# Products by columns in a two-layer decoder trunk: three products of 256 columns per k tile, or one of 512 and one of 256 with a join

## The chip, the cores and the metric

The kernel runs on one core of one Trainium2 chip. The metric is device time in microseconds of that core, median of several runs. The engines are named as the profile names them: PE (TensorE matmul), PEld (its weight loads), DVE (VectorE), ACT (ScalarE), POOL (GpSimd) and SP (SyncE, which issues the DMAs here).

## What is computed

The reference is a decoder trunk of two layers on x of 256 tokens by 1024 features, all in float32.

```python
for i in range(DEPTH):                      # DEPTH = 2
    y = chunked_gmlp(x, ...) if i % 2 == 0 else moba_attention(x, ...)
    x = layer_norm(DN_ALPHA * x + y, ln_mix_g[i], ln_mix_b[i])
    y = conv_ffn(x, f_w_up[i], f_conv_w[i], f_conv_b[i], f_w_down[i])
    x = layer_norm(DN_ALPHA * x + y, ln_ffn_g[i], ln_ffn_b[i])

# chunked_gmlp: z = gelu(x @ w_in); u, v = split(z); v = layer_norm(v); mix v over positions; (u * v) @ w_out
# moba_attention: q, k, v = x @ w_qkv; 16 heads of 64; softmax with a position bias; @ w_o
# conv_ffn: h = x @ w_up (1024 to 5632); causal convolution of width 3; gelu(g) * val; @ w_down
```

## The kernel before

**Two parts of every operand.** Each weight and each x is split into a high part (rounded to the matmul's fp32r) and a low part (what the rounding left). A product is three matmuls: high by high, high by low, low by high. For weights, ACT writes `whi` and DVE writes `wlo` from a raw chunk in SBUF; for x the tiles are `xth` and `xtl`, kept transposed (128 features of a k tile on the partitions, tokens along them); there are KT = 8 k tiles.

**The stream of weights.** 1 MB chunks come in the order a_v, a_u, a_out, f_up0 (22 chunks), f_dn0 (11), b_v, b_qk (8), b_o, f_up1, f_dn1, through two raw buffers, and each is split into two sub-chunks of 1024 columns. The rings of high and low parts hold five chunks; a chunk is fetched and split when PE has spent the one five before it (`spent`, L376).

**By rows and by columns.** Some stages work by rows (`rows_step`, L520): x is the stationary operand, 512 columns of the weights move, and the result has tokens on the partitions. The others work by columns (`cols_times`, L528): a 128 x 128 piece of the weights is stationary, the 256 tokens of x move, and 256 columns of one PSUM bank collect one block of 128 output features, over 8 k tiles of three matmuls each. By columns go a_u (8 blocks), chunks 2 to 21 of each f_up (two blocks each, gate and value) and b_qk (two blocks for each of 8 pairs of heads). PSUM has eight banks, taken in turn; each block of columns takes one.

**What reads a block.** In a_u (L639) ACT applies Gelu from PSUM. In f_up, `gate` (L655) reads each block three times in PSUM: ACT Identity with bias and scale (the first tap), and two scalar_tensor_tensor on DVE (the other taps); then Gelu on ACT, a product on DVE, and a split by ACT and DVE into `rr`. In b_qk, `project` (L735) makes from the bank a copy of the first 128 tokens, a high part (ACT) and a low part (DVE); scores, softmax, transposes and the products with v follow for a pair some pairs behind.

**What sets the order.** The kernel records all operations and then orders them itself (`Plan.emit`, L122): a list scheduler with a cost for every operation gives each engine its fixed order, which the engine then works through first in, first out. PE's long products keep the recorded order; transposes and the attention's small products fill in between. Operations of DVE and ACT are taken by due time. Numbers of the cost model are not times of the chip.

The layout of the transposed x before is (t, k, c): tokens in two halves t of 128, in each the 8 k tiles. A moving operand of 256 tokens is therefore read in two runs of 128.

Of the kernel before, what the change touches and what calls it, by code (L numbers as in the profile page):

```python
# [11 lines left out]
F32 = mybir.dt.float32  # L12
F32R = mybir.dt.float32r
# [210 lines left out]
def trunk_kernel(ctx: ExitStack, tc: tile.TileContext, a: dict, out: bass.AP):  # L224
# [13 lines left out]
    xth, xtl = Ring(tiles("xth", 1, KT * S, F32R)), Ring(tiles("xtl", 1, KT * S, F32R))  # L238
# [154 lines left out]
    def xt_view(b):  # L393
        return b.ap.rearrange("p (t k c) -> p t k c", t=NT, k=KT)
# [3 lines left out]
    xv32 = xT32.ap.rearrange("p (t k c) -> p t k c", t=NT, k=KT)  # L398

    def load_xt(k, n, rank):  # L400
        load(xv32[:, :, k:k + n, :], a["xT"][:, :, k:k + n, :], [(xT32, [(t, j) for t in range(NT) for j in range(k, k + n)])],
             rank=rank)
        for t in range(NT):
            parts = [(t, j) for j in range(k, k + n)]
            split((xh, parts, xt_view(xh)[:, t, k:k + n, :]), (xl, parts, xt_view(xl)[:, t, k:k + n, :]),
                  (xT32, parts, xv32[:, t, k:k + n, :]), by="dve" if k == 0 else "act")
# [188 lines left out]
    def gmlp():  # L595
# [37 lines left out]
        for g in range(GROUPS):  # L633
# [5 lines left out]
            act(us[g].ap, b.ap[:, :S], AF.Gelu_apprx_tanh, [b], [us[g]], psum=True, table="gelu")  # L639
# [7 lines left out]
    def conv_up(layer, h, l):  # L647
# [58 lines left out]
    def moba(h, l, scr):  # L706
# [5 lines left out]
        qkring = [Places("ff", (j * 2 * P, j * 2 * P + P), P) for j in range(2)]  # L712
# [22 lines left out]
        def project(i, j):  # L735
# [4 lines left out]
            src, (th, tl) = b.ap[:, at2:at2 + n], (x.new() for x in qkparts[j])  # L740
            act(t.ap, b.ap[:, :P], AF.Copy, [b], [t], scale=scale, psum=True)
# [178 lines left out]
```

## Time and profile before

| | us |
|---|---|
| timed runs | 584.77, 582.66, 583.03 |
| median | 583.03 |
| span of the profiled execution, first to last instruction | 580.6 |
| PE busy / DVE busy / ACT busy in it | 565.9 / 453.5 / 340.9 |

The page gives the span of the profiled execution and no other time of it; the median of the timed runs lies 2.4 us above that span. TensorE's granted clock has a mean of 0.996 of full speed.

Rows of groups read: line, engine, operation, out<-in by tile names, shapes, count, then busy us, mean ns of one, idle time of the engine before them and what ended it. Rows of the timeline read: start, duration, engine, line, operation, count; x4 are four in a row merged into one line. PE's matmuls are pipelined and drawn longer than the distance from one to the next, so starts are to be compared, not lengths. Rows of the windows read: stretch, its length, busy us (and count) of PE, PEld, DVE, ACT and POOL, granted clock, DMA share, GB/s. Rows of waits read: engine, tile and line, what it waited for, us in total, times, longest.

PE's stages in the profiled execution are about: a_v to 31, a_u to 57, a_out with its LayerNorm to 81, f_up0 to 210 (by columns from 93), f_dn0 to 271, b_v to 293, b_qk to 358, b_o to 385, f_up1 to 513 (by columns from 397), f_dn1 to 573.

### The profile page before, as it was taken

The page shows a single profiled execution, that of the slowest core. Times are in us where ns is not written, and L with a number is a line of the kernel's source. Part 1 is how long each engine was busy: PE and PEld are TensorE (multiplying, and loading weights), DVE is VectorE, ACT ScalarE, POOL GpSimd, SP SyncE. Part 2 cuts the span into 40 slices and gives each one's busy share as a digit, 9 for nine tenths or more (in the row PEclk, how much of TensorE's full clock was granted, in tenths as well). Part 3 has the DMA queues.
Part 4 walks back from the last instruction along what each step waited for, and adds up shares of the span by engine and source line. Part 5 has one row for each costly group of instructions (what it writes and reads, how often), then busy time and mean ns, then how long its engine had stood idle before and what let it go on. Part 6 is the DMA issues. An engine that isn't in the chain of part 4 may idle for free.

```text
span 580.6 us, 9855 instructions
## 1 busy us (share of the span) xinstructions
PE 565.9 (97%) x3850; PEld 521.7 (90%) x3850; DVE 453.5 (78%) x845; ACT 340.9 (59%) x620; POOL 11.2 (2%) x17
## 2 busy tenths in 40 slices
PE   6999999999999999999999999999999999999994
PEld 4799889999999998888899988889999999988884
DVE  4599889988989874448978988889989888874326
ACT  5556567866676654325667875577767766653200
POOL 0020010000000000001000000000000000000001
PEclk9999999999999999999999999999999999999998
DMA  7997536667555555450665542416755654545202
GB/s 254 345 346 279 189 128 217 222 214 266 194 200 213 196 205 201 171 208 23 242 268 176 182 164 73 148 71 227 290 209 218 215 189 179 207 163 210 73 1 72
DMA packets 20138, 111.01 MB, mean 191 GB/s; under 512 B 2251, under 2 KB 6268, under 8 KB 7676
## 3 DMA queue, kind: packets, MB, share of 16 engines
q1 hardware_dynamic: 20092, 110.39, 52.9%
q8 instruction: 30, 0.49, 0.3%
q14 instruction: 16, 0.13, 0.1%
HBM read 109.31 MB, written 1.07 MB: 190 GB/s over the span
## 4 chain that ended last, share of the span: by engine, by line
PE 93%; DMA 3%; DVE 1%; ACT 1%; issue 1%; SPq 0%; DVEq 0%; ACTq 0%
PE bank L293 91%; DMA raw<-in_a_v 2%; PE bank L299 2%; DMA raw<-in_b_o 1%; ACT whi L305 1%; DVE wlo L311 1%; DVE x L315 0%; SPq L322 0%; ACT rr L305 0%; DVE ff L773 0%; ACT ff L305 0%; DVE stat L461 0%; DVEq L916 0%; DVE qk L315 0%; ACT qk L305 0%
## 5 line engine op out<-in xcount | busy, mean ns | idle before, releaser
L311 DVE TENSOR_TENSOR wlo<-raw,whi 128x1024 fp32r<-128x1024 f32 (+1 forms) x212 | 229.8, 1099 | 56.6 <-ACT whi L305 56.1
L305 ACT ACTIVATE whi<-raw 128x1024 fp32r<-128x1024 f32 (+1 forms) x212 | 196.3, 956 | 79.6 <-PE bank L293 52.1
L293 PE MATMUL bank<-xth,whi 128*128 128x256 f32 x832 | 237.1, 285 | 0.0
L293 PE MATMUL bank<-xth,wlo 128*128 128x256 f32 x832 | 235.4, 283 | 0.0
L293 PE MATMUL bank<-xtl,whi 128*128 128x256 f32 x832 | 235.4, 283 | 0.0
L293 PEld LDWEIGHTS bank<-xth,whi 128*128 128x128 f32 x832 | 159.5, 192 | 1.5 <-issue 0.6
L293 PEld LDWEIGHTS bank<-xtl,whi 128*128 128x128 f32 x832 | 159.6, 192 | 0.2
L293 PEld LDWEIGHTS bank<-xth,wlo 128*128 128x128 f32 x832 | 159.6, 192 | 0.0
L293 PE MATMUL bank<-whi,rr 128*128 128x512 f32 (+1 forms) x528 | 152.9, 371 | 0.0
L293 PEld LDWEIGHTS bank<-whi,rr 128*128 128x128 f32 x528 | 96.4, 188 | 16.6
L293 PE MATMUL bank<-wlo,rr 128*128 128x512 f32 (+1 forms) x264 | 97.7, 370 | 0.0
L315 DVE SCALAR_TENSOR_TENSOR ff<-bank,convc,ff 128x254 f32<-128x254 f32 (+1 forms) x176 | 80.5, 476 | 13.9 <-ACT ff L305 12.9
L305 ACT ACTIVATE ff<-bank,convc 128x256 f32<-128x256 f32 x88 | 48.7, 561 | 48.7 <-PE bank L293 37.2
L293 PEld LDWEIGHTS bank<-wlo,rr 128*128 128x128 f32 x264 | 49.8, 189 | 8.2
L293 PE MATMUL bank<-whi,xth 128*128 128x512 f32 x96 | 39.1, 408 | 5.4 <-DVE xth L328 5.0
L293 PE MATMUL bank<-wlo,xth 128*128 128x512 f32 x96 | 38.6, 402 | 1.0 <-DVE wlo L311 0.9
L293 PE MATMUL bank<-whi,xtl 128*128 128x512 f32 x96 | 38.1, 397 | 0.0
L305 ACT ACTIVATE ff<-bank,lncol 128x128 f32<-128x128 f32 x48 | 18.9, 459 | 28.7 <-PE bank L299 28.7
L315 DVE SCALAR_TENSOR_TENSOR x<-x,bank 128x512 f32<-128x512 f32 (+1 forms) x24 | 14.3, 596 | 25.0 <-PE bank L293 24.9
L293 PEld LDWEIGHTS bank<-whi,xth 128*128 128x128 f32 x96 | 18.5, 193 | 9.4 <-ACT whi L305 5.8
L293 PEld LDWEIGHTS bank<-wlo,xth 128*128 128x128 f32 x96 | 18.4, 192 | 5.7 <-DVE wlo L311 2.4
L305 ACT ACTIVATE rr<-ff 128x256 fp32r<-128x256 f32 x52 | 21.1, 407 | 2.8 <-DVE ff L311 2.7
(51 smaller groups left out, 350.6 us busy)
## 6 DMA issues: line engine op xcount, KB each, us to landing
raw<-in_f_up SPq DMA_DIRECT2D x44, 1024.0 KB, 4.8
raw<-in_f_dn SPq DMA_DIRECT2D x22, 1024.0 KB, 4.8
raw<-in_b_qk SPq DMA_DIRECT2D x8, 1024.0 KB, 4.8
lnrow<-in_lnrow SPq DMA_DIRECT2D x5, 1024.0 KB, 7.2
raw<-in_a_u SPq DMA_DIRECT2D x4, 1024.0 KB, 5.4
raw<-in_a_out SPq DMA_DIRECT2D x4, 1024.0 KB, 5.2
raw<-in_b_v SPq DMA_DIRECT2D x4, 1024.0 KB, 4.7
raw<-in_b_o SPq DMA_DIRECT2D x4, 1024.0 KB, 5.1
```

Of the source, the lines that this page charges most:

```text
L293: nc.tensor.matmul(o, l, x, start=start, stop=stop)
L299: nc.tensor.transpose(o, x, ident.ap)
L305: plan.op("act", ns, lambda: nc.scalar.activation(o, x, func, **kw), r, w, table=table)
L311: dve(70 + 1.04 * flat(x), lambda: nc.vector.tensor_tensor(o, x, y, op=op), r, w)
L315: lambda: nc.vector.scalar_tensor_tensor(o, x, s, y, op0=op0, op1=op1), r, w)
```

## The change

The high and low parts of the transposed x become the two halves of one tile `xt2`, and its layout becomes (k, t, c), so that the 256 tokens of a k tile lie together. In `cols_times` one matmul of 512 columns multiplies the high weights with both parts of x: high by high falls into the first half of the bank and high by low into the second. A matmul of 256 columns adds low by high into the first half. A new helper, `join`, brings the halves together in SBUF: ACT copies the second half, DVE adds the first (with a scale for q). Gelu in a_u, the three taps in f_up (chunks 2 to 21) and the splits in b_qk then read the joined block in SBUF; `hring` is a ring of eight places for the blocks of f_up. In b_qk the kept block is 256 wide instead of 128. xT is loaded in the new layout, with one split for both halves of the tokens. Work by rows is as before, with the new view of x.

```diff
+    xt2 = sb.tile([P, 2 * KT * S], F32R, name="xt2")
+    xth, xtl = Ring([xt2[:, :KT * S]]), Ring([xt2[:, KT * S:]])
+    xboth = xt2.rearrange("p (x k s) -> p x k s", x=2, k=KT)
...
-        return b.ap.rearrange("p (t k c) -> p t k c", t=NT, k=KT)
+        return b.ap.rearrange("p (k t c) -> p t k c", t=NT, k=KT)
...
-        for t in range(NT):
-            parts = [(t, j) for j in range(k, k + n)]
-            split((xh, parts, xt_view(xh)[:, t, k:k + n, :]), (xl, parts, xt_view(xl)[:, t, k:k + n, :]),
-                  (xT32, parts, xv32[:, t, k:k + n, :]), by="dve" if k == 0 else "act")
+        parts, sl = [(t, j) for t in range(NT) for j in range(k, k + n)], slice(k * S, (k + n) * S)
+        load(xT32.ap[:, sl], a["xT"][:, sl], [(xT32, parts)], rank=rank)
+        split((xh, parts, xh.ap[:, sl]), (xl, parts, xl.ap[:, sl]), (xT32, parts, xT32.ap[:, sl]),
+              by="dve" if k == 0 else "act")
...
     def cols_times(b, h, l, hi, lo):
-        o = b.ap[:, :S].rearrange("p (t c) -> p t c", t=NT)
-        hv, lv = xt_view(h), xt_view(l)
+        both = b.ap.rearrange("p (x s) -> p x s", x=2)
         for k in range(KT):
             ks, parts = slice(k * P, (k + 1) * P), [(t, k) for t in range(NT)]
-            mms([(o, w.ap[:, ks], x[:, :, k, :], k == 0 and j == 0, k == KT - 1 and j == 2)
-                 for j, (w, x) in enumerate([(hi, hv), (hi, lv), (lo, hv)])],
+            mms([(both, hi.ap[:, ks], xboth[:, :, k, :], k == 0, False),
+                 (b.ap[:, :S], lo.ap[:, ks], xboth[:, 0, k, :], False, k == KT - 1)],
                 [(hi, [k // 2]), (lo, [k // 2]), (h, parts), (l, parts)], [b])
...
+    def join(b, c, scale=1.0):
+        act(c.ap, b.ap[:, S:], AF.Copy, [b], [c], scale=scale, psum=True)
+        if scale == 1.0:
+            tt(c.ap, b.ap[:, :S], c.ap, ALU.add, [b, c], [c])
+        else:
+            stt(c.ap, b.ap[:, :S], scale, c.ap, ALU.mult, ALU.add, [b, c], [c])
...
-            act(us[g].ap, b.ap[:, :S], AF.Gelu_apprx_tanh, [b], [us[g]], psum=True, table="gelu")
+            join(b, us[g])
+            act(us[g].ap, us[g].ap, AF.Gelu_apprx_tanh, [us[g]], [us[g]], table="gelu")
...
-                srcs.append((b, b.ap[:, :S]))
+                c = hring.new()
+                join(b, c)
+                srcs.append((c, c.ap))
...
-            act(t.ap, b.ap[:, :P], AF.Copy, [b], [t], scale=scale, psum=True)
-            act(th.ap, src, AF.Copy, [b], [th], scale=scale, psum=True)
-            stt(tl.ap, src, scale, th.ap.bitcast(F32), ALU.mult, ALU.subtract, [b, th], [tl])
+            join(b, t, scale)
+            th, tl = (x.new() for x in qkparts[j])
+            split((th, [0], th.ap), (tl, [0], tl.ap), (t, [0], t.ap[:, at2:at2 + n]))
```

**How the fixed orders move.** The first place is DVE's queue in the middle of f_up0, about one chunk. `wlo` are low parts of later weights, `convc` marks the taps of the convolution, `ff<-ff` is the product of gate and value, `rr` its low part. Before:

```order
L311 TENSOR_TENSOR wlo6_81<-raw0_85,whi6_71 128x1024
L311 TENSOR_TENSOR ff_105<-ff_105 128x256
L311 TENSOR_TENSOR wlo7_82<-raw0_85,whi7_72 128x1024
L315 SCALAR_TENSOR_TENSOR ff_105<-bank0_106,convc_117,ff_105 128x255
L315 SCALAR_TENSOR_TENSOR ff_105<-bank1_107,convc_117,ff_105 128x255
L315 SCALAR_TENSOR_TENSOR ff_105<-bank0_106,convc_117,ff_105 128x254
L315 SCALAR_TENSOR_TENSOR ff_105<-bank1_107,convc_117,ff_105 128x254
```

And in the changed kernel, where `ff<-bank7,ff` and `ff<-bank0,ff` are the additions of two joins:

```order
L313 TENSOR_TENSOR wlo6_81<-raw1_86,whi6_71 128x1024
L313 TENSOR_TENSOR wlo7_82<-raw1_86,whi7_72 128x1024
L313 TENSOR_TENSOR ff_104<-bank7_112,ff_104 128x256
L317 SCALAR_TENSOR_TENSOR ff_104<-ff_104,convc_116 128x255
L313 TENSOR_TENSOR rr_103<-ff_104,rr_103 128x256
L313 TENSOR_TENSOR ff_104<-bank0_105,ff_104 128x256
L317 SCALAR_TENSOR_TENSOR ff_104<-ff_104,convc_116 128x254
```

Each block now has an addition that reads the bank, and the taps name the bank no more; the taps of a block stand further behind its product on PE.

The second place is DVE's queue as a_u begins, where the LayerNorm of v (`stat`, `lnrow`) and the first spatial products (`ff<-bank,ff` before) stand. Before:

```order
L311 TENSOR_TENSOR ff_105<-bank0_106,ff_105 128x256
L315 SCALAR_TENSOR_TENSOR ff_105<-ff_105,stat0_92,lnrow0_91 128x512
L315 SCALAR_TENSOR_TENSOR ff_105<-ff_105,stat1_93,lnrow0_91 128x512
L311 TENSOR_TENSOR ff_105<-ff_105 128x256
L315 SCALAR_TENSOR_TENSOR ff_105<-ff_105,stat0_92,lnrow0_91 128x256
L315 SCALAR_TENSOR_TENSOR ff_105<-ff_105,stat1_93,lnrow0_91 128x256
L311 TENSOR_TENSOR ff_105<-bank4_110,ff_105 128x256
L311 TENSOR_TENSOR wlo6_81<-raw0_85,whi6_71 128x1024
```

And in the changed kernel, where banks 4 to 7 are the first four blocks of a_u and bank 0 the first spatial product:

```order
L313 TENSOR_TENSOR ff_104<-bank4_109,ff_104 128x256
L313 TENSOR_TENSOR ff_104<-bank5_110,ff_104 128x256
L313 TENSOR_TENSOR ff_104<-bank6_111,ff_104 128x256
L313 TENSOR_TENSOR ff_104<-bank7_112,ff_104 128x256
L313 TENSOR_TENSOR ff_104<-bank0_105,ff_104 128x256
L317 SCALAR_TENSOR_TENSOR ff_104<-ff_104,stat0_91,lnrow0_90 128x512
L317 SCALAR_TENSOR_TENSOR ff_104<-ff_104,stat1_92,lnrow0_90 128x512
L313 TENSOR_TENSOR ff_104<-ff_104 128x256
L313 TENSOR_TENSOR wlo6_81<-raw0_85,whi6_71 128x1024
```

Four additions stand together ahead of the rest of the LayerNorm and of the first low part of a_out; the other four of a_u stand between later rows.

The third place is ACT's queue in b_qk, around the blocks of one pair of heads. `qk256` and `qk128` are high parts of k and of q, `smax` marks the exponentials, `rr<-bank` the high parts of transposed weights of the softmax. Before:

```order
L305 ACTIVATE ff_105<-bank4_110 128x128
L305 ACTIVATE qk25601_124<-bank4_110 128x256
L305 ACTIVATE rr_104<-bank5_111 128x384
L305 ACTIVATE rr_104<-bank6_112 128x384
L305 ACTIVATE whi3_68<-raw0_85 128x1024
L305 ACTIVATE whi4_69<-raw1_86 128x1024
L305 ACTIVATE qk12800_119<-bank0_106 128x128
L305 ACTIVATE ff_105<-bank0_106 128x128
```

And in the changed kernel:

```order
L307 ACTIVATE ff_104<-bank4_109 128x256
L307 ACTIVATE rr_103<-bank5_110 128x384
L307 ACTIVATE qk25601_123<-ff_104 128x256
L307 ACTIVATE rr_103<-bank6_111 128x384
L307 ACTIVATE whi2_67<-raw0_85 128x1024
L307 ACTIVATE ff_104<-bank0_105 128x256
L307 ACTIVATE whi3_68<-raw0_85 128x1024
L307 ACTIVATE qk12800_118<-ff_104 128x128
```

The high part no longer stands beside the copy out of the bank: it waits for DVE's addition, and another operation of ACT stands between the two.

More of the change, by code (lines that the diff above doesn't have):

```diff
@@ L237, in trunk_kernel @@
     raws = Ring(tiles("raw", RAWS, CH))
-    xth, xtl = Ring(tiles("xth", 1, KT * S, F32R)), Ring(tiles("xtl", 1, KT * S, F32R))
+    xt2 = sb.tile([P, 2 * KT * S], F32R, name="xt2")
+    xth, xtl = Ring([xt2[:, :KT * S]]), Ring([xt2[:, KT * S:]])
+    xboth = xt2.rearrange("p (x k s) -> p x k s", x=2, k=KT)
     xs_ = tiles("x", NT, D)
@@ L651, in conv_up @@
         gring, yring = Places("ff", (4 * S, 5 * S), S), Places("ff", (6 * S, 8 * S), HALF)
+        hring = Places("ff", (3456, 3712, 3968, 4224, 6 * S, 7 * S, 8 * S, 9 * S), S)
         cc = convc.ap.rearrange("p (n f c) -> p n f c", n=DEPTH, c=4)
@@ L658, in gate @@
                 cw, c = cc[:, layer, j * FT + i, :], cring[j].new()
-                act(c.ap, o, AF.Identity, [b, convc], [c], bias=cw[:, 3:4], scale=cw[:, 2:3], psum=True)
+                act(c.ap, o, AF.Identity, [b, convc], [c], bias=cw[:, 3:4], scale=cw[:, 2:3], psum=i < 2)
                 for d in (1, 2):
@@ L711, in moba @@
         pring = [Places("rr", [4 * n4 + (2 * j + x) * pw for x in range(2)], pw) for j in range(2)]
-        qkring = [Places("ff", (j * 2 * P, j * 2 * P + P), P) for j in range(2)]
+        qkring = [Places("ff", (j * 2 * S, j * 2 * S + S), S) for j in range(2)]
         qkparts = [[Ring(tiles(f"qk{n}{j}", 2, n, F32R)) for j in range(2)] for n in (P, S)]
@@ L739, in project @@
             n, at2, scale = (P, P, DH ** -0.5) if j == 0 else (S, 0, 1.0)
-            src, (th, tl) = b.ap[:, at2:at2 + n], (x.new() for x in qkparts[j])
-            act(t.ap, b.ap[:, :P], AF.Copy, [b], [t], scale=scale, psum=True)
-            act(th.ap, src, AF.Copy, [b], [th], scale=scale, psum=True)
-            stt(tl.ap, src, scale, th.ap.bitcast(F32), ALU.mult, ALU.subtract, [b, th], [tl])
+            join(b, t, scale)
+            th, tl = (x.new() for x in qkparts[j])
+            split((th, [0], th.ap), (tl, [0], tl.ap), (t, [0], t.ap[:, at2:at2 + n]))
             t = (t, th, tl)
@@ L758, in both @@
             def both(o, seq):
-                return [(bank2[hh].ap[:, o[0]:o[1]], x.ap[hh * DH:(hh + 1) * DH], y.ap[hh * DH:(hh + 1) * DH],
+                return [(bank2[hh].ap[:, o[0]:o[1]], x[hh * DH:(hh + 1) * DH], y[hh * DH:(hh + 1) * DH],
                          n == 0, n == len(seq) - 1) for n, (x, y) in enumerate(seq) for hh in range(2)]
-            mms(both((0, P), [(q0, k0)]) + both((P, P + S), [(qh, kh), (qh, kl), (ql, kh)]),
+            mms(both((0, P), [(q0.ap[:, :P], k0.ap[:, :P])]) + both((P, P + S), [(x.ap, y.ap) for x, y in ((qh, kh), (qh, kl), (ql, kh))]),
                 [q0, qh, ql, k0, kh, kl], bank2, fill=True)
@@ L870, in _layout @@
         "x": f(x.reshape(NT, P, D).transpose(1, 0, 2)),
-        "xT": f(x.reshape(NT, P, KT, P).transpose(3, 0, 2, 1)),
+        "xT": f(x.reshape(NT, P, KT, P).transpose(3, 2, 0, 1).reshape(P, -1)),
         "a_v": by_rows(w_in[:, D:]),
```

3 lines of the change are left out of this document (removed).

## The prediction

> **What bounds the kernel now.** I read the page first: its busy shares and the chain that ended last.
>
> ```profile
> span 580.6 us, 9855 instructions
> PE 565.9 (97%) x3850; PEld 521.7 (90%) x3850; DVE 453.5 (78%) x845; ACT 340.9 (59%) x620; POOL 11.2 (2%) x17
> PE 93%; DMA 3%; DVE 1%; ACT 1%; issue 1%; SPq 0%; DVEq 0%; ACTq 0%
> ```
>
> A busy PE is not yet a PE at its peak, so the second view is the list of waits, for PE alone.
>
> ```profile
> PE bank L293 <- DVE xth L328: 5.0, 1, 5.0
> PE bank L293 <- DVE wlo L311: 0.9, 2, 0.8
> PE bank L293 <- DVE qk L315: 0.7, 1, 0.7
> PE bank L293 <- ACT whi L305: 0.4, 1, 0.4
> ```
>
> 7.0 us in all, 5.0 of them before the first product. So the time is the sum of the distances between products, and the third view is PE's timeline, first inside a product by columns of f_up0 (256 wide, x read in two runs of 128 columns), then in f_dn0 (512 wide, then 256 wide, each read in one run).
>
> ```profile
> 102.81 0.28 PE L293 MATMUL bank<-xth,wlo 128*128 128x256 f32 x1
> ...
> 105.93 0.28 PE L293 MATMUL bank<-xtl,whi 128*128 128x256 f32 x1
> ```
> ```profile
> 254.83 0.39 PE L293 MATMUL bank<-wlo,rr 128*128 128x512 f32 x1
> ...
> 265.03 0.39 PE L293 MATMUL bank<-wlo,rr 128*128 128x512 f32 x1
> 266.48 0.28 PE L293 MATMUL bank<-wlo,rr 128*128 128x256 f32 x1
> ...
> 270.44 0.28 PE L293 MATMUL bank<-wlo,rr 128*128 128x256 f32 x1
> ```
>
> From 102.81 to 105.93 there are 26 products: 3.12 / 26 = 0.120 us each, though each is drawn 0.28 long. From 254.83 to 265.03 there are 45 products (15 steps of three): 10.20 / 45 = 0.2267 us. From 266.48 to 270.44 there are 33: 3.96 / 33 = 0.120 us. So 256 more columns cost 0.2267 - 0.120 = 0.1067 us, and what is left, 0.120 - 0.1067 = 0.0133 us, is paid once per product, whatever its width; two runs cost no more than one.
>
> **The gain.** A step of cols_times was three products of 256 columns, 3 x 0.120 = 0.360 us. It becomes one of 512 and one of 256: 0.2267 + 0.120 = 0.3467. The columns are the same; one fixed part of 13.3 ns goes.
>
> ```profile
> L293 PE MATMUL bank<-xth,whi 128*128 128x256 f32 x832 | 237.1, 285 | 0.0
> ```
>
> There are 832 steps (8 in a_u, 16 in b_qk, 40 in each f_up, times 8 k tiles): 832 x 0.0133 = 11.1 us, of which a_u 0.85, b_qk 1.7 and each f_up 4.3. This is the first term, -11.1.
>
> A rule of the Trainium skill speaks against it ("TensorE: Matmul & The Clock Gate", section "Back-to-back issue gap"): the distance warm is the columns by 2.4 GHz plus about 2.5 ns. By that the step would save 2.5 ns and the whole 2.1 us; the trace does not agree, since its fixed part is 13.3 ns, and the sum goes by the trace.
>
> **What the change adds: a join for each of 104 columns.** ACT copies 256 elements out of PSUM, DVE adds 256, and only then come Gelu, Identity or the split as before. Prices, from the groups kept apart by shape:
>
> ```profile
> L311 DVE TENSOR_TENSOR wlo<-raw,whi 128x1024 fp32r<-128x1024 f32 x164 | 199.0, 1221 | 54.7 <-ACT whi L305 54.3
> L315 DVE SCALAR_TENSOR_TENSOR ff<-bank,convc,ff 128x255 f32<-128x255 f32 x88 | 41.2, 478 | 13.3 <-ACT ff L305 12.9
> L311 DVE TENSOR_TENSOR ff<-bank,ff 128x256 f32<-128x256 f32 x8 | 3.2, 417 | 0.0
> L305 ACT ACTIVATE ff<-bank 128x256 f32<-128x256 f32 x8 | 3.0, 381 | 10.2 <-PE bank L293 10.2
> L305 ACT ACTIVATE whi<-raw 128x1024 fp32r<-128x1024 f32 x164 | 169.5, 1054 | 71.1 <-PE bank L293 52.1 <-DMA raw<-in_f_up 7.8 <-DMA raw<-in_a_v 3.7
> ```
>
> The add is the operation of the third row, 0.417 us, the copy that of the fourth (there with Gelu), 0.381. But DVE's instructions overlap at their ends, as its timeline in f_up0 shows, at a place where it is never idle:
>
> ```profile
> 98.93 2.35 DVE L311 TENSOR_TENSOR wlo<-raw,whi 128x1024 fp32r<-128x1024 f32 x2
> 101.20 1.64 DVE L315 SCALAR_TENSOR_TENSOR ff<-bank,convc,ff 128x255 f32<-128x255 f32 x4
> 102.76 0.41 DVE L311 TENSOR_TENSOR ff<-ff 128x256 f32<-128x256 f32 x1
> 103.09 1.22 DVE L311 TENSOR_TENSOR wlo<-raw,whi 128x1024 fp32r<-128x1024 f32 x1
> ...
> 121.58 1.22 DVE L311 TENSOR_TENSOR wlo<-raw,whi 128x1024 fp32r<-128x1024 f32 x1
> ```
>
> From start to start a low part takes 2.27 / 2 = 1.135, a tap of the convolution 1.56 / 4 = 0.39, an addition of 256 takes 0.33. So a join costs DVE 0.33 where it is behind. All 104 cost it 34 us, and what counts is whether PE sees any of that, stage by stage.
>
> **f_up0 and f_up1 (80 of the joins).** The windows:
>
> ```profile
> 95.00:211.00 116.00, 116.00 (x958) 115.01 (x957) 104.44 (x180) 79.73 (x132) 0.00 (x0) 1.00 0.62 220
> 98.95:121.50 22.55, 22.55 (x190) 22.55 (x189) 22.55 (x40) 16.59 (x28) 0.00 (x0) 1.00 0.65 234
> 292.00:346.00 54.00, 53.45 (x442) 50.66 (x441) 45.40 (x140) 40.18 (x105) 0.00 (x0) 1.00 0.53 186
> ```
>
> In the second row DVE is full. The low part at 98.93 is the first of chunk 5 and that at 121.58 the first of chunk 10 (ten 1024-wide ones stand between): 22.65 / 5 = 4.53 us a chunk, two of the LayerNorm's leftovers included. With two joins: 4.53 + 0.66 = 5.19. PE needs 16 steps a chunk, 5.76 before, 5.55 after. DVE stays below, at 94%, so its queue does not grow; but it no longer catches up by 1.2 us a chunk, only by 0.36. How far ahead it is:
>
> ```profile
> 93.15 0.28 PE L293 MATMUL bank<-xth,whi 128*128 128x256 f32 x1
> ```
>
> PE begins chunk 2 at 93.15, and after three chunks of 5.76 it needs chunk 5 at 110.4; that chunk's first low part is ready at 98.93 + 1.2 = 100.1. The lead is 10.3 us, and it covers the joins: behind an add that waits for its copy stand the next low parts in DVE's queue, and PE waits for these only when 10.3 us are used up. Were that cover gone, each chunk would cost PE what DVE is over 5.55. Bounds here: none below zero, since PE waits for nothing between 95 and 211; above, two chunks' joins each, 1.3 in each f_up. I take 0. The banks are no bound: a column takes one of eight as before, and a join ends sooner than two taps.
>
> ACT is no bound either: 79.73 of 116 us, plus 40 copies of 0.38 and a little for Identity from SBUF, 96 of 111.7.
>
> **a_u into a_out (8 joins).** DVE's last work for a_out, and PE's first product there:
>
> ```profile
> 63.23 0.76 DVE L311 TENSOR_TENSOR rr<-ff,rr 128x256 fp32r<-128x256 f32 x2
> 57.47 0.40 PE L293 MATMUL bank<-whi,rr 128*128 128x512 f32 x1
> 58.86 0.60 PE L293 MATMUL bank<-ff 128*128 128x128 f32 x4
> L311 DVE TENSOR_TENSOR wlo<-raw,whi 128x1024 fp32r<-128x1024 f32 x10 | 12.0, 1221 | 1.1 <-ACT whi L305 1.1
> ```
>
> The low part of the last group is ready at 63.99 and is first needed with the 40th product of 512 columns: 57.47 + 0.4 for the fill + 39 x 0.2267 = 66.7. PE comes 0.85 earlier, so 1.9 us of lead stand against 8 x 0.33 = 2.7 us of joins, of which DVE can take 1.1 where it now idles for ScalarE (last row, from 40 to 65). Between 0 and 0.8 us; I take 0.2, near the lower end, since 2.7 - 1.1 = 1.6 is under 1.9.
>
> **b_qk (16 joins).** DVE is at 45.40 of 54 us, and ACT at 40.18. Some 13 of the joins lie in this stretch: 49.7 of 52.5, 95%, on the engine through which scores, softmax and transposes run one after another. Where PE waits there today, ACT had been held by a weight chunk:
>
> ```profile
> 343.42 2.01 ACT L305 ACTIVATE whi<-raw 128x1024 fp32r<-128x1024 f32 x2 [2.13 <-DMA raw<-in_b_o]
> ```
>
> That is the wait of 0.7 for qk in the list above; it may go or grow, as raw buffers are released at other times. Below: -0.7. Above: all 16 adds seen by PE, 16 x 0.33 = 5.3. I take +1.5, about two more waits of that size, nearer to the lower end because PE waited once in 54 us with DVE at 84%.
>
> **The rest.**
>
> ```profile
> L305 ACT ACTIVATE ff<-ff 128x256 f32<-128x256 f32 x44 | 18.0, 409 | 4.6 <-DVE rr L311 4.5
> L315 DVE SCALAR_TENSOR_TENSOR ff<-ff,stat,lnrow 128x256 f32<-128x256 f32 x8 | 3.6, 477 | 0.0
> 11.16 6.95 DMA raw<-in_a_v
> ```
>
> Identity and splits that read SBUF instead of PSUM change by 0.409 - 0.381 = 0.03 us, on an engine with room; a tap whose source is SBUF costs the same, 0.477 against 0.478. xT arrives in longer pieces with one split instead of two, but the chain of waits goes there through a transfer of a_v (last row), so I take 0, between -0.3 and +0.3.
>
> **Sum.** -11.1 + 0 + 0.2 + 1.5 = -9.4 us; the span goes from 580.6 to 571.2. The page gives no time but the span; the median of the timed runs, 583.03, lies 2.4 above it, as what lies around the first and the last instruction, and that stays: 573.6.
>
> **Rivals.**
>
> The gain is not there: the fixed 13.3 ns belong to each 256 columns written or to each far-apart run read, so a wide product costs 2 x 0.120. Then the step stays at 0.360 and 1.7 us of waits are left: 584.7. Against it: two runs in f_up0 cost what one run costs in f_dn0, and 512 columns cost 0.2267. For it: no product of before reads two runs of 256 that lie 2048 elements apart. By the page's 2.5 ns it would be 583.03 - 2.1 + 1.7 = 582.6, which is no change too. 0.07 for both.
>
> VectorE is the bound: the joins wait. On ACT a copy can stand behind a weight split of 1.054 us, and the add at the head of DVE's queue with it; if every join idles so, a chunk takes DVE 5.19 + 2.1 = 7.3. From chunk 5 to 21 that is 17 x 1.74 = 29.6 against 10.3 of lead: 19.3 us in each f_up, 573.6 + 38.6 = 612, slower. It begins to cost at 0.48 us of idle a join (5.19 + 0.96 = 6.15, 17 x 0.6 = 10.3) and makes the kernel slower by over 0.5% from 0.66 (17 x 0.97 = 16.4, 6.1 us in each f_up). Against it: where DVE is behind, it does not idle at all (22.55 of 22.55), because copies are then done long before. 0.06.
>
> Part of the gain is lost in b_qk and at the stage borders, the upper bounds of the terms together: 5.3 + 0.8 + 2.6 = 8.7 in place of 1.7, 580.6; this case runs from 576.5 to there. 0.13.
>
> **Numbers.** The forecast's own case, 570.8 to 576.5, has 0.74: down to there if the 0.7 goes and the start gains 0.3 (583.03 - 12.1, a little less). The range reaches up into the partial loss, to 578.5, and leaves out under 2 in 10. A measurement of this kernel tells about 0.5%, 2.9 us. Faster by more than that 0.87, within it 0.07, slower 0.06.
>
> **What would show it.** In the new profile: PE's starts in f_up0 0.3467 apart for each pair of products; DVE near 94% in both f_up stages with no wait of PE for wlo or for a bank; PE's waits for qk, ff or rr of some 2 us between 270 and 360. It is wrong if a pair takes 0.36, or if PE waits in f_up for DVE by more than 3 us.

## The result and the profile after

| kernel | median us | runs (lowest to highest) | ratio to before, 95% interval |
|---|---|---|---|
| before | 582.88 | 4 (582.66 to 584.77) | |
| changed | 577.1 | 4 (576.63 to 578.55) | 0.9902 [0.9883, 0.9921] |

The change saves 0.98%, 5.7 us by the ratio; forecast were 9.4. The profiled execution took 577.02 us with a span of 575.3, so 1.7 us lie around the span, and not 2.4 (1.7 to 2.2 in all executions with both numbers). The three rows of the page that answer to those shown of before:

```profile
span 575.3 us, 8284 instructions
PE 559.9 (97%) x3018; PEld 475.2 (83%) x3018; DVE 483.6 (84%) x944; ACT 372.9 (65%) x705; POOL 11.6 (2%) x17
PE 92%; DVE 3%; DMA 2%; ACT 1%; issue 0%; SPq 0%; DVEq 0%; ACTq 0%
```

PE has 832 products fewer and is busy for the same share of the span, 97%; VectorE went from 453.5 to 483.6 us. First PE's timeline in the middle of f_up0, then in the middle of f_up1; all rows left out alternate in the same way:

```profile
149.72 0.39 PE L295 MATMUL bank<-xt,whi 128*128 128x512 f32 x1
149.95 0.27 PE L295 MATMUL bank<-xt,wlo 128*128 128x256 f32 x1
...
151.80 0.39 PE L295 MATMUL bank<-xt,whi 128*128 128x512 f32 x1
```
```profile
449.76 0.40 PE L295 MATMUL bank<-xt,whi 128*128 128x512 f32 x1
450.00 0.28 PE L295 MATMUL bank<-xt,wlo 128*128 128x256 f32 x1
...
451.88 0.40 PE L295 MATMUL bank<-xt,whi 128*128 128x512 f32 x1
```

In the middle of f_up0 six pairs take 151.80 - 149.72 = 2.08 us, 0.3467 a pair: the forecast to the digit. In f_up1 six take 2.12, 0.3533 a pair, with the same instructions and without a wait. That is 6.7 ns more a pair, and 320 pairs: 2.1 us that no step of the prediction had.

The short value does not hold to the end of f_up0 either. Two small products of another kind (`bank<-ff`, 384 wide) come between at 189.33, and behind them:

```profile
189.12 0.28 PE L295 MATMUL bank<-xt,wlo 128*128 128x256 f32 x1
189.33 0.81 PE L295 MATMUL bank<-ff 33*16 33x384 f32 x2
190.08 0.50 PE L295 MATMUL bank<-xt,whi 128*128 128x512 f32 x1
...
196.18 0.40 PE L295 MATMUL bank<-xt,whi 128*128 128x512 f32 x1
...
198.30 0.40 PE L295 MATMUL bank<-xt,whi 128*128 128x512 f32 x1
```

Six pairs take 2.12 us here too, and so it stays for the last 42 pairs, to 205.37; the 272 pairs from 94.59 to 188.89 took 0.3467 each. Parts of a_u and b_qk also run near the long value (the 22 pairs of b_qk from 289.05 take 352.7 each). Summed over all pairs that follow one another undisturbed, the time above 0.3467 a pair is 0.2 us in a_u, 0.3 in f_up0, 0.4 in b_qk and 2.1 in f_up1: 3.0 us.

The windows (columns as before: stretch, length, PE, PEld, DVE, ACT, POOL, clock, DMA share, GB/s) of f_up0 by columns, of f_up1 by columns, and of the stretch from the last block of b_qk to the last product of the heads; then that last stretch in the kernel before:

```profile
97.50:185.00 87.50, 87.50 (x507) 76.44 (x506) 82.96 (x150) 66.73 (x120) 0.00 (x0) 1.00 0.63 225
400.00:510.00 110.00, 110.00 (x621) 95.30 (x621) 101.67 (x183) 84.42 (x152) 0.00 (x0) 1.00 0.59 211
350.98:365.15 14.17, 13.99 (x75) 10.73 (x73) 13.77 (x39) 11.51 (x30) 0.00 (x0) 1.00 0.62 220
```
```profile
357.71:368.62 10.91, 10.91 (x63) 8.92 (x62) 9.91 (x29) 6.62 (x19) 0.00 (x0) 1.00 0.54 192
```

VectorE is at 95% in f_up0 and 92% in f_up1 (94% forecast), PE never idle there, at full clock. But behind b_qk VectorE is at 97%, and the stretch is 3.3 us longer than before. PE's waits:

```profile
PE bank L295 <- DVE rr L313: 1.0, 3, 0.7
PE bank L295 <- ACT rr L307: 1.0, 1, 1.0
PE bank L295 <- DVE wlo L313: 0.4, 1, 0.4
PE bank L295 <- ACT xt L307: 0.2, 1, 0.2
```

The wait of 0.7 for qk is gone; new are waits for `rr`, at two places. The first is in a_out, PE's row and VectorE's:

```profile
64.91 0.39 PE L295 MATMUL bank<-wlo,rr 128*128 128x512 f32 x1
66.00 0.74 PE L295 MATMUL bank<-whi,rr 128*128 128x512 f32 x2 [0.70 <-DVE rr L313]
66.58 0.40 PE L295 MATMUL bank<-wlo,rr 128*128 128x512 f32 x1
```
```profile
64.39 1.22 DVE L313 TENSOR_TENSOR wlo<-raw,whi 128x1024 fp32r<-128x1024 f32 x1
65.52 0.76 DVE L313 TENSOR_TENSOR rr<-ff,rr 128x256 fp32r<-128x256 f32 x2
```

From 64.91 to 66.58 is 1.67 us for three products in place of 0.68: 1.0 lost, while VectorE ends the low parts of the last groups at 66.28, 2.3 us later than before (63.99). The second place is in b_o, at the last pair of heads (`bank<-rr` are its products with v, the products behind them need its result):

```profile
363.27 0.40 PE L295 MATMUL bank<-whi,rr 128*128 128x512 f32 x1
363.67 0.50 PE L295 MATMUL bank<-rr 128*128 128x512 f32 x1
364.34 1.08 PE L295 MATMUL bank<-rr 128*128 128x512 f32 x5 [0.18 <-DVE rr L313]
366.39 0.50 PE L295 MATMUL bank<-whi,rr 128*128 128x512 f32 x1 [0.96 <-ACT rr L307]
366.73 0.40 PE L295 MATMUL bank<-wlo,rr 128*128 128x512 f32 x1
367.29 0.73 PE L295 MATMUL bank<-whi,rr 128*128 128x512 f32 x2 [0.16 <-DVE rr L313]
367.85 0.39 PE L295 MATMUL bank<-wlo,rr 128*128 128x512 f32 x1
```

The six products of the heads are three of 512 and three of 256 columns. From 363.27 to 367.85 PE makes 11 products that would take 8 x 0.227 + 3 x 0.120 = 2.18 us, and it takes 4.58: 2.4 us are lost here, and 0.5 more at 387 in the same way. In the kernel before the loss at this place is 0; the six products, drawn as one row, are followed after 1.03 us, and bare they take 1.04:

```profile
367.71 1.20 PE L293 MATMUL bank<-rr 128*128 128x512 f32 x6
368.74 0.40 PE L293 MATMUL bank<-whi,rr 128*128 128x512 f32 x1
```

So three sums are to be explained: 3.0 us of PE's pace (2.1 of them in f_up1), 2.4 at the last heads, 1.0 in a_out.

### The profile page after: what moved, and what is told of

Same layout as the page of the kernel before. It is cut to its first block, busy times and chain, and to the rows that moved or that the text cites. A ratio compares the mean times of both kernels' runs of the same rounds, so it can differ in the third digit from the quotient of the medians.

```text
span 575.3 us, 8284 instructions
## 1 busy us (share of the span) xinstructions
PE 559.9 (97%) x3018; PEld 475.2 (83%) x3018; DVE 483.6 (84%) x944; ACT 372.9 (65%) x705; POOL 11.6 (2%) x17
## 4 chain that ended last, share of the span: by engine, by line
PE 92%; DVE 3%; DMA 2%; ACT 1%; issue 0%; SPq 0%; DVEq 0%; ACTq 0%
PE bank L295 90%; DMA raw<-in_a_v 2%; PE bank L301 2%; DVE wlo L313 1%; ACT whi L307 1%; DVE ff L313 1%; DVE x L317 0%; DVE rr L313 0%; SPq L324 0%; ACT ff L307 0%; ACT rr L307 0%; DVE stat L460 0%; DVEq L925 0%; ACT xt L307 0%; DVE stat L463 0%
## 5 line engine op out<-in xcount | busy, mean ns | idle before, releaser
L295 PE MATMUL bank<-xt,whi 128*128 128x512 f32 x832 | 295.3, 399 | 0.0
L295 PE MATMUL bank<-xt,wlo 128*128 128x256 f32 x832 | 232.5, 279 | 0.0
L307 ACT ACTIVATE whi<-raw 128x1024 fp32r<-128x1024 f32 (+1 forms) x212 | 194.9, 956 | 53.2 <-PE bank L295 30.2
L295 PEld LDWEIGHTS bank<-xt,whi 128*128 128x128 f32 x832 | 156.2, 188 | 37.7 <-issue 0.6
L295 PEld LDWEIGHTS bank<-xt,wlo 128*128 128x128 f32 x832 | 156.8, 188 | 0.2
L307 ACT ACTIVATE ff<-bank 128x256 f32<-128x256 f32 (+1 forms) x108 | 41.4, 387 | 57.1 <-PE bank L295 44.6
L317 DVE SCALAR_TENSOR_TENSOR ff<-ff,convc 128x255 f32<-128x255 f32 (+1 forms) x160 | 72.2, 477 | 0.4 <-ACT ff L307 0.3
L295 PE MATMUL bank<-whi,xt 128*128 128x512 f32 x192 | 63.7, 402 | 5.3 <-ACT whi L307 5.1
L313 DVE TENSOR_TENSOR ff<-bank,ff 128x256 f32<-128x256 f32 x104 | 42.8, 421 | 16.8 <-ACT ff L307 16.1
L307 ACT ACTIVATE ff<-ff,convc 128x256 f32<-128x256 f32 x80 | 46.3, 593 | 6.7 <-DVE ff L313 6.3
L295 PE MATMUL bank<-wlo,xt 128*128 128x512 f32 x96 | 38.6, 402 | 0.4 <-DVE wlo L313 0.4
```

The lines of the kernel that those rows point to most:

```text
L295: nc.tensor.matmul(o, l, x, start=start, stop=stop)
L307: plan.op("act", ns, lambda: nc.scalar.activation(o, x, func, **kw), r, w, table=table)
L313: dve(70 + 1.04 * flat(x), lambda: nc.vector.tensor_tensor(o, x, y, op=op), r, w)
L317: lambda: nc.vector.scalar_tensor_tensor(o, x, s, y, op0=op0, op1=op1), r, w)
```

## The experiments

All ratios are to the kernel before, run in the same set. "Loss at the last heads" is what PE's distances there exceed the bare ones by, in each run as just done. `cols_three` below is the old way (three products of 256 into one half) in the new layout of x. The code shown is in part shortened, and ... marks what is left out. The pace of a stage is told from the one execution of a run that has a profile; "f_up0 at 346.7" means its pairs up to some 189 us, since the last 42 to 48 pairs of f_up0 take 353.3 in every profile of a kernel with wide and narrow products in turn.

**The grouped order.** In `cols_times` all wide products of a block come first:

```diff
-        for k in range(KT):
-            mms([(both, hi[k], x_both[k], ...), (first_half, lo[k], x_high[k], ...)], ...)
+        for k in range(KT):
+            mms([(both, hi[k], x_both[k], ...)], ...)
+        for k in range(KT):
+            mms([(first_half, lo[k], x_high[k], ...)], ...)
```

> Edit: in every block of columns of the changed kernel the eight wide products are issued first and the eight 256-wide ones behind them, in place of one wide and one narrow in turn. All work is kept. In the changed kernel a pair of products takes 346.7 ns in f_up0 and 353.3 ns in f_up1, though the instructions are the same. Theory (the rhythm of alternating widths on PE settles in one of two states by the moment of entry): without the alternation a step is 226.7 + 120 ns = 346.7 ns in every stage, f_up1 gets back about 2.1 us, a_u and b_qk some 0.5 together, and the span goes from 575.3 to about 572.7. Rival (the joins on VectorE and ScalarE take PSUM or SBUF bandwidth from PE in f_up1): the joins are still there, a step in f_up1 stays at 353 ns and the span at 575.3 +-0.5. Second rival: PE's rhythm in f_up1 is a chance of one execution, then f_up1 may come out at 346.7 in any of the runs of this set, grouped or not.

Measured: 576.83 us, 0.9908 [0.9891, 0.9925], span 575.5. PE's timeline in f_up1, four blocks (rows of eight products each):

```profile
450.72 1.12 PE L295 MATMUL bank<-xt,wlo 128*128 128x256 f32 x8
451.68 2.00 PE L295 MATMUL bank<-xt,whi 128*128 128x512 f32 x8
...
459.10 1.12 PE L295 MATMUL bank<-xt,wlo 128*128 128x256 f32 x8
```

Three blocks of eight steps in 8.38 us are 349.2 ns a step, in f_up0 too. The long value of 353.3 is gone with all joins in place, which speaks against the joins as its cause; but the expected 346.7 is not reached. So f_up1 gains 1.3 us and f_up0 loses 0.5, and b_qk got a new order with a wait of 1.08 us behind it, at 357.7, which took the rest. By itself half an answer.

**a_u undone.**

```diff
-            cols_times(b, xh, xl, *sub("a_u", g // 2, g % 2))
+            cols_three(b, xh, xl, *sub("a_u", g // 2, g % 2))
...
-            join(b, us[g])
-            act(us[g].ap, us[g].ap, AF.Gelu_apprx_tanh, [us[g]], [us[g]], table="gelu")
+            act(us[g].ap, b.ap[:, :S], AF.Gelu_apprx_tanh, [b], [us[g]], psum=True, table="gelu")
```

> Edit: a_u alone goes back to three products of 256 per k tile into one half of the bank, with Gelu read from PSUM; f_up and b_qk stay wide with joins. All work is kept. Theory (the wait of 1.09 us before PE's product at 64.9 us in a_out comes from the eight joins of a_u in VectorE's queue): the wait goes, 0.85 us of the gain is given back, and the time falls or rises by under 0.3 us: 576.9. Rival (that wait has another cause, the weight stream or the order of ScalarE): it stays and the time rises by 0.85 to about 578.

Measured: 574.42 us, 0.9866 [0.9847, 0.9886]. The wait in a_out is gone, as expected (PE's list of waits has 5.0 for the start, 1.0 and 0.3 at the last heads, and no other). But the time fell by 2.1 us more by the ratio than for the whole change, and the reason is elsewhere, in f_up1, whose code was not touched:

```profile
449.67 0.39 PE L295 MATMUL bank<-xt,whi 128*128 128x512 f32 x1
...
451.75 0.39 PE L295 MATMUL bank<-xt,whi 128*128 128x512 f32 x1
```
```profile
400.00:510.00 110.00, 110.00 (x629) 95.91 (x627) 104.93 (x190) 85.05 (x156) 0.00 (x0) 1.00 0.61 216
```

Six pairs in 2.08 us, 346.7 ns; 629 products in 110 us where the changed kernel makes 621. So f_up1 can have either pace with the same instructions and the same joins.

**b_qk undone.** As in a_u, with the copy, the high part and the low part made from PSUM as before.

> Edit: b_qk alone goes back to three products of 256 per k tile into one half of the bank, with the copy, high part and low part made from PSUM; a_u and f_up stay wide with joins. All work is kept. Theory (the 2.3 us that PE loses between 363 and 367.3 us, in the last heads of b_o, and 0.4 at 387, come from the joins of b_qk, which make ScalarE late so that four pieces of weight splits stand ahead of the last heads' high parts): these waits go, 1.7 us of the gain is given back, and the time falls by about 0.7 to 576.4. Rival (ScalarE is late there because of the weight stream or of the new order in general): the waits stay and the time rises by 1.7 to 578.8.

Measured: 574.74 us, 0.9872 [0.985, 0.9893]. The loss at the last heads falls from 2.4 to 0.9 and the 0.5 at 387 goes; in a_out PE still loses 1.1; f_up1 is at 346.7. The theory holds for most of the 2.4 and not for the rest. Nor is the 0.5 at 387 tied to b_qk by this: it is gone with a_u undone, too. The four profiles of the alternating order that have this wait (the changed kernel, twice, and the runs with the last pair undone and with extra products below) are the four with 353.3 in f_up1, and the other six have neither; whether one brings the other is not shown.

**Only the new layout and loading of x.** All three stages by `cols_three`, no joins.

> Edit: all three stages go back to three products of 256 without joins; only the new layout and loading of the transposed x (k, t, c, one tile for both parts) stay. All work is kept. Theory (the 0.87 us by which the first dense product comes earlier is the work of the new loading; products by rows and columns cost the same in both layouts): 582.9 - 0.9 = 582.0, PE's steps 360 ns everywhere. Rival (the earlier start is a chance of the order): 582.9. Second rival (the read in one run instead of two was part of the gain): steps under 360 ns, and the time clearly under 582.

Measured: 582.2 us, 0.9997 [0.9984, 1.0011]. Reading one run instead of two brings nothing, and neither does the loading. The earlier start in the profile of the changed kernel is scatter: over the 14 profiles the 96th product starts between 30.0 and 31.4 us (before 31.1, changed 30.2, the changed kernel again 31.0).

**Wide products, no joins.** It leaves out the addition of the high-by-low part in all products by columns; the cut shows f_up, and a_u and b_qk read the bank likewise.

```diff
-                c = hring.new()
-                join(b, c)
-                srcs.append((c, c.ap))
+                srcs.append((b, b.ap[:, :S]))
```

> Edit: the wide products stay, and the joins go: Gelu in a_u, the taps in f_up and the splits in b_qk read the first half of the bank in PSUM, as before the change. It leaves out the high-by-low part of all products by columns. It measures PE's gain alone. Theory (joins cost PE 1.0 us in a_out and some 2.5 us in the last heads of b_o and after; in f_up nothing; PE's rhythm in each f_up stage takes 346.7 or 353.3 ns a step): no wait of PE at 65 us, none at 363 to 367 us, 582.2 - 11.1 - 0.7 (start) = 570.4 with the short rhythm in both stages, 572.5 or 574.6 with the long one in one or both. Rival (PE's losses in after come from PE being early against the stream of weights, joins or not): waits at those places stay, with no join in the queues, and the time is 574 or more with the short rhythm in both.

Measured: 572.34 us, 0.9835 [0.9823, 0.9848], 9.6 us below before. Both f_up stages are at 346.7 (f_up0 again with a tail, 48 pairs at 353.3 from 188.15 to 205.11, though no join is in this kernel), the wait in a_out is gone, and 0.9 us stay at the last heads. 11.1 - 0.9 = 10.2 lies within the interval (8.9 to 10.3); the start's 0.7 of the expectation did not come. So at the last heads 0.9 can be lost without any join, and the other 1.5 of the 2.4 come with them.

**Joins, no wide products.** High by low goes to the second half of the bank in a product of its own.

```diff
-            mms([(both, hi[k], x_both[k], ...), (first_half, lo[k], x_high[k], ...)], ...)
+            mms([(first_half, hi[k], x_high[k], ...), (second_half, hi[k], x_low[k], ...),
+                 (first_half, lo[k], x_high[k], ...)], ...)
```

> Edit: three products of 256 per k tile as before, but high by low goes to the second half of the bank, and all 104 joins are made. All work is kept. It measures the joins alone, with PE at 360 ns a step. Theory: f_up costs nothing (5.19 us of VectorE work against 5.76 a chunk), a_out up to 0.3 (PE comes 0.85 later than with wide products), the last heads of b_o about 2.3, since their chain is longer by two steps whatever PE does: 582.2 + 2.5 = 584.7. Rival (the joins cost PE only because PE became faster): 582.2 +-0.5.

Measured: 584.72 us, 1.0051 [1.0039, 1.0063]: the joins alone cost 3.0 us, 2.2 of it at the last heads, 0.9 in a_out, and nothing in f_up, where PE's products stay 0.120 apart. The rival (joins cost only because PE became faster) falls.

**Only the last pair of heads undone.**

```diff
+            three = i == PAIRS - 1
+            (cols_three if three else cols_times)(b, h, l, *sub("b_qk", i, j))
```

> Edit: of b_qk only the last pair of heads (2 of 16 blocks) goes back to three products and to splits from PSUM; the rest is the changed kernel. All work is kept. Theory (the loss of 2.3 us at the last heads of b_o is the chain of the last pair: copy, addition, high part and low part hop between ScalarE and VectorE and stand each time behind a weight split of 1.0 to 1.2 us, so the scores come 3 us later after the end of b_qk): the waits at 363 to 367 us go, 0.2 us is given back, about -2.1 in that stretch. Rival (the load of all 16 joins makes both queues late): under 0.7 of it goes. In the time: 577.0 - 2.1 = 574.9, or 572.8 if PE's rhythm in f_up1 comes out short besides.

Measured: 576.85 us, 0.9907 [0.9889, 0.9925]. The loss stays at 2.3. The last pair's own longer chain is not the cause: that theory falls, and its rival (the load of all joins) stands. In a_out 0.5 is lost here. What the load does is seen in the stretch from the last block of b_qk to the start of the last heads' products, counting the low parts of weights alone (columns: stretch, length, then PE, PEld and DVE with `wlo`; DVE's is the third), for before, the changed kernel and this run:

```profile
357.71:367.71 10.00, 4.20 (x11) 1.97 (x11) 2.61 (x4) 1.00 0.59 210
```
```profile
350.98:363.67 12.69, 5.37 (x14) 2.45 (x13) 5.47 (x5) 1.00 0.59 199
```
```profile
350.53:363.04 12.51, 5.36 (x14) 2.53 (x14) 4.84 (x5) 1.00 0.60 214
```

2.9 us (2.2 in this run) of low parts that stood within b_qk before now stand in VectorE's queue between the steps of the last pair. That joins bring them there is seen where nothing else differs: with the layout alone there are 2.6 us of them, with joins and no wide products 4.9. PE has 39 products of b_o that do not need this pair; it had made 30 of them when the pair was ready before, and has made all 39 now. So the 9 x 0.227 = 2.04 us that had covered the splits of the pair's result are used up.

**Extra products.** Ahead of chunks 6, 9, 12, 15 and 18 of both f_up stages one to five products of 256 columns are put in, whose results are overwritten.

```diff
+                if j == 0 and i in KNOCK:              # {6: 1, 9: 2, 12: 3, 15: 4, 18: 5}
+                    mms([(first_half, hi[0], x_high[0], True, True)] * KNOCK[i], ...)
```

> Edit: the changed kernel with one to five extra products of 256 columns ahead of chunks 6, 9, 12, 15 and 18 of both f_up stages (15 in each stage, 0.12 us each, 3.6 us in all; their results are overwritten). Theory (the rhythm of 512 and 256 columns in turn has two states, 346.7 and 353.3 ns a step, and which one holds is set by where PE stands when the alternation begins): the step changes between the two values at some of these places and keeps its value between them, in stages in which it was constant before. Rival (something in f_up1 slows PE: the joins, the transfers, the data): f_up0 stays at 346.7 and f_up1 at 353.3 throughout. Time between 577.0 + 3.6 - 2.1 and 577.0 + 3.6 + 2.1.

Measured: 581.19 us, 0.9988 [0.9975, 1.0001]. PE's timeline in f_up0 around chunk 12 (x4 at 149.52 are the three extra products and the first wide one behind them):

```profile
147.09 0.39 PE L296 MATMUL bank<-xt,whi 128*128 128x512 f32 x1
...
149.17 0.39 PE L296 MATMUL bank<-xt,whi 128*128 128x512 f32 x1
149.40 0.28 PE L296 MATMUL bank<-xt,wlo 128*128 128x256 f32 x1
149.52 0.75 PE L296 MATMUL bank<-xt,whi 128*128 128x256 f32 x4
...
155.17 0.40 PE L296 MATMUL bank<-xt,whi 128*128 128x512 f32 x1
...
157.29 0.40 PE L296 MATMUL bank<-xt,whi 128*128 128x512 f32 x1
```

Up to 149.17 six pairs take 2.08 us; behind the extra products they take 2.12 (155.17 to 157.29), and it stays so to the end of the stage. The other nine interruptions changed nothing: at chunks 6 and 9 of f_up0 the pace stayed short, at 15 and 18 long, and f_up1 was at 353.3 throughout. So the pace changed at an interruption of PE's stream, in a stage with the same joins and transfers on both sides of it, and the rival falls. The changed kernel itself shows the same at 189 us, and so does the kernel without any join: the joins are not needed for the long value. Why three products changed it there and five elsewhere did not is open, and with one change in ten places the theory (the moment at which the alternation begins) is not shown.

**The changed kernel again.**

> The changed kernel once more, without an edit. If the rhythm of PE in f_up1 is set by the program (the order and the moments at which PE enters the stage), a new execution shows the same 353.3 ns a step in f_up1 and 346.7 in f_up0, and the time is 576.5 to 577.5. If it is a chance of the execution, f_up1 can come out at 346.7 and single runs 2.1 us apart.

Measured: 576.46 us, 0.99 [0.9875, 0.9925]; the profiled execution again has 353.3 in f_up1 and 346.7 in f_up0, span 575.5. The six times lie at 574.99, 575.29, 575.66 and at 577.27 (the profiled one), 577.56, 579.62. A gap of that size fits two paces of f_up1 among the executions of one program; as only one of them has a profile, this is not shown.

**Only f_up wide.** a_u and b_qk both undone.

> Edit: a_u and b_qk both go back to three products and to readers in PSUM; only f_up stays wide with joins. All work is kept. Theory (in a_u and b_qk the joins cost PE about what the wide products save: 1.0 against 0.85 and 1.65 against 1.7): no wait of PE at 65 us, at most 0.7 us lost at the last heads of b_o, and 582.3 - 8.5 = 573.8 with the short rhythm in both f_up stages, 575.9 with the long one in one of them, against 577 of the whole change. Rival (the gain of a_u and b_qk is kept in the whole change): 2.5 us above it, 579.5.

Measured: 572.95 us (572.11 to 573.16), 0.9833 [0.9815, 0.985]: 9.7 us below before, and 3.5 below the whole change in the same set, without overlap of the single times. No wait in a_out, no loss at the last heads, both stages at 346.7. The 3.5 us come out of the terms: the changed kernel's second profile loses 0.5 in a_out, 2.4 at the last heads, 0.5 at 387, 2.1 by the pace of f_up1 and 0.6 by that of a_u and b_qk, and its wide products there save 2.55: 3.55. So 2.1 of the 3.5 are the pace of f_up1 and no work saved. The stretch behind b_qk and PE at the last heads:

```profile
352.70:363.62 10.92, 10.92 (x64) 8.94 (x63) 9.92 (x29) 6.63 (x19) 0.00 (x0) 1.00 0.59 194
```
```profile
362.70 1.20 PE L295 MATMUL bank<-rr 128*128 128x512 f32 x6
363.74 0.40 PE L295 MATMUL bank<-whi,rr 128*128 128x512 f32 x1
```

VectorE's 9.92 of 10.92 us is before's value, and the six products take 1.04, their bare 3 x 0.227 + 3 x 0.120. This is the fastest version with the whole computation.

**The additions of b_qk on GpSimd.** ScalarE copies both halves, GpSimd adds; a_u by three products.

```diff
-            join(b, t, scale)
+            act(d.ap, b.ap[:, S:], AF.Copy, [b], [d], scale=scale, psum=True)
+            act(t.ap, b.ap[:, :S], AF.Copy, [b], [t], scale=scale, psum=True)
+            plan.op("pool", 500, lambda: nc.gpsimd.tensor_tensor(t.ap, t.ap, d.ap, op=ALU.add), [t, d], [t])
```

> Edit: a_u by three products, as in the run with a_u alone undone; f_up and b_qk wide; in b_qk ScalarE copies both halves of the bank and GpSimd adds them in SBUF, so VectorE has no join there. All work is kept. Theory (VectorE's load: the 16 additions of b_qk, some 5.3 us, push low parts of later weights behind the end of b_qk, where VectorE then is at 97% while the last pair's chain goes through it): VectorE's share between the last block of b_qk and the last product of the heads falls from 97 to about 90%, PE's loss at the last heads from 2.1 to about 0.7, and the time from 574.4 to 573.0. Rival (the chain through more operations is the cause, on whichever engines; it is longer here by one copy): the loss stays at 2 or grows, 574.4 or more.

Measured: 575.24 us, 0.9874 [0.9857, 0.9892], against 0.9866 for the run with a_u undone: no gain, where 1.4 us were expected. VectorE's share behind b_qk is 83%, its low parts there are 3.8 us in place of the 4.9 of that run, and the loss at the last heads is 1.6 in place of 2.4; but new waits at 333, 340 and 358 us (0.3, 0.4 and 0.6) took that back. The 16 additions take GpSimd 0.92 us each in the mean, as the profile draws them:

```profile
L560 POOL TENSOR_TENSOR ff<-ff 128x256 f32<-128x256 f32 x16 | 14.7, 917 | 69.6 <-ACT ff L307 58.6 <-DVE ff L808 8.9 <-PE bank L295 2.1
```

Neither theory alone gives this run: the loss fell, but to 1.6 and not to 0.7, and the time is the rival's. That load and chain both count is the likely reading, not a shown one.

**Half of each small stage.** a_u wide in groups 0 to 3, b_qk in pairs 0 to 3.

> Edit: wide with joins in the first half of each small stage and three products in the second: a_u groups 4 to 7 and b_qk pairs 4 to 7 by three products, the rest and f_up wide. All work is kept. Theory (VectorE's load, with time to catch up after the joins): no wait of PE at 65 us, the loss at the last heads between 0.7 and 1.2, 1.27 us of the gain in a_u and b_qk kept: 573.8 - 1.3 + 0.3 = 572.8 with the short rhythm in both f_up stages, 574.9 with the long one in one. Rival (any join in b_qk brings the new order of the queues and with it the loss of 2): 574.2 with the short rhythm.

Measured: 573.91 us, 0.9843 [0.9825, 0.9862]. No wait in a_out: four joins fit. At the last heads PE loses 1.7, more than expected: the joins end four pairs earlier, and 4.8 us of low parts still stand in the last pair's stretch. Both f_up stages are at 346.7, and the time lies between the theory's 572.8 and the rival's 574.2.

The last heads in all runs, by what stands in VectorE's queue (us of `wlo` between the last block of b_qk and the last heads' first product, read from the windows as above):

| run | joins in b_qk | wlo there | PE's loss |
|---|---|---|---|
| before; layout alone; f_up only | 0 | 2.6 | 0 |
| b_qk undone; no joins at all | 0 | 4.1; 3.9 | 0.9 |
| additions on GpSimd | 0 on VectorE | 3.8 | 1.6 |
| half | 8 | 4.8 | 1.7 |
| last pair undone; joins alone; a_u undone | 14; 16; 16 | 4.8; 4.9; 4.9 | 2.3; 2.2; 2.4 |
| grouped | 16 | 5.1 | 2.3 |
| changed, both times; extra products | 16 | 5.5 | 2.4 |

The loss rises with the joins, but the low parts alone do not order it: about 4.8 us of them go with 1.7 in one run and 2.4 in another, and 3.8 on the way over GpSimd with more loss than 4.1. So the load is one part of the cause, and the length of the chain, or the place of the low parts in it, is another that no run here takes apart.

## Why the prediction was right, and where it was off

The sign, the range and the main mechanism held; the size was 9.4 forecast against 5.7. The forecast's own case, 570.8 to 576.5, did not come: 577.1 lies in the part of the range that was added for the third rival (part of the gain lost in b_qk and at the stage borders, chance 0.13). It got there by 3.0 us of PE's pace, which neither the forecast nor a rival had; that a range made wider for another reason held it was in part luck.

- **The gain (-11.1).** Right in its mechanism. The fixed part of 13.3 ns goes once per step where a pair takes 0.3467, as in most of f_up0; at 0.3533 only half of it goes. With the other joins away (f_up only) 640 x 0.0133 = 8.5 us were due and 9.7 came, with an interval of 8.7 to 10.8; less 0.3 for the tail of f_up0, and with the wait of 0.7 for qk that this run no longer has, 8.9 were due. The rule of the Trainium skill ("TensorE: Matmul & The Clock Gate", section "Back-to-back issue gap"), 2.5 ns per product, would have given 640 x 0.0025 = 1.6 us; the runs do not agree. The section gives this rule for a single product apart from a stream, and for a stream of weight loads and products about 131 ns at 512 columns; the 226.7 of these traces are neither.
- **That a pair costs 0.3467 everywhere.** This step failed for f_up1 (353.3 ns, 2.1 us in the stage) and in parts of f_up0, a_u and b_qk (0.9 together). The prediction took the two distances from stages in which one width follows itself, and had no row of two widths in turn. The long value comes without any join, and PE goes over to it at an interruption of its stream; what sets it is not known.
- **f_up0 and f_up1: joins cost 0.** Right. With joins alone PE keeps 0.120 from product to product in both stages. VectorE idles 0.15 us an addition for ScalarE's copy, far under the 0.48 at which the second rival begins to cost:

```profile
L313 DVE TENSOR_TENSOR ff<-bank,ff 128x256 f32<-128x256 f32 x104 | 42.8, 421 | 16.8 <-ACT ff L307 16.1
L307 ACT ACTIVATE ff<-bank 128x256 f32<-128x256 f32 x104 | 39.3, 380 | 55.6 <-PE bank L295 43.1 <-DVE ff L317 3.6 <-issue 3.2
```

  (16.1 / 104 = 0.15; the first row holds 96 joins and 8 of a_u's spatial products, the 8 joins of q with their scale are another operation.) The two durations, 0.421 and 0.380, are those forecast from other rows, 0.417 and 0.381.
- **a_u into a_out (+0.2, at most 0.8).** Too low: 1.0 in the first profile, 0.5 in the second, and between 0.5 and 1.1 in the other runs with all joins of a_u. The term was mis-sized: 2.7 us of joins less 1.1 of idle time would be 1.6, and VectorE ended 2.3 us later, which is more than the 1.9 of lead. The idle time for weight splits was used up as forecast, but VectorE idled anew for the copies of the joins, 1.9 us from 40 to 66.3 (1.4 in the second profile), and the sum had nothing for that:

```profile
L313 DVE TENSOR_TENSOR ff<-bank,ff 128x256 f32<-128x256 f32 x16 | 6.2, 418 | 1.9 <-ACT ff L307 1.9
```

  With a_u or its second half undone the wait is gone.
- **b_qk (+1.5, -0.7 to 5.3).** The place failed, the size was near: the wait of 0.7 for qk inside b_qk went, and 2.4 + 0.5 us came at the last heads and just behind, 2.2 in all. The joins did not make PE wait where they stand; they moved weight splits behind the stage, into a chain that PE had been covering by 2.04 us. How much of the 2.4 is the splits and how much the chain stays open.
- **The rest (0).** Right, and the -0.9 at the start of the first profile is no part of it: the layout alone gives 0.9997.
- **2.4 us around the span.** It is 1.7 to 2.2; the rest was the distance of one execution from the median.

Together, with the first profile: -11.1 + 3.0 + 1.0 + 2.4 + 0.5 - 0.7 = -4.9, against -5.7 with an interval of -6.8 to -4.6; what is left is of the size of the scatter of the start.

What stays open: why the low parts behind b_qk are 4.1 and 3.9 us in two runs without joins there and 2.6 in a third, though b_qk undone and f_up only have the same code in b_qk: the scheduler's order differs, and by which of its rules was not followed. What the wait at 387 comes from. And what in PE sets the pace.

## What to carry to other kernels

Work that is added to an engine with room need not cost where it is done: it can push the engine's deferrable work to the next place where a chain is short of cover, so look behind the stage, and count how many products PE has left there that do not need the chain. Undo a change stage by stage: here a_u gave back in waits (0.5 to 1.0 us) about what its wide products save (0.85), b_qk with the wait at 387 more (2.9 against 1.7), and the version with f_up alone is the fastest. But read the profile before the gain is put down to the stage that was undone: 2.1 us of it came from PE's pace in another stage. A pitch measured on products of one width is not the pitch of two widths in turn.

## What the runs showed of the hardware that was not expected

PE, without any wait and at full granted clock, has two paces for products of 512 and 256 columns in turn, each with its own weights: 346.7 and 353.3 ns a pair. It keeps the one it has fallen into (for 316 pairs on end in f_up1) and may change it where the turn is interrupted: behind two small products of 384 columns it went from 346.7 to 353.3 in f_up0 of every profile that was at the short value there, and behind three extra products of 256 once, while nine other interruptions by one to five products left it as it was. Eight wide products followed by eight narrow ones take 349.2 a pair. Products of 256 alone, and steps of three of 512, had one pace in every profile, 120.0 and 226.7 ns.
